# Layer 0 from an unnormalized, transposed x; the norm's per-token factor applied to q, k and v

## The chip, the cores and the metric

The kernel runs on one core of a Trainium2 chip. A core has a matrix engine (TensorE, "PE" in the profile, with its weight loads as "PEld"), VectorE ("DVE"), ScalarE ("ACT"), GpSimd ("POOL") and SyncE ("SP"), which here issues all transfers. The engines run side by side, each through its own list of instructions in order, and wait for one another by semaphores. The metric is the device time of one execution in microseconds; lower is better.

## The reference

A decoder trunk of two layers works on x with 256 tokens and 1024 channels, all in float32. What bears on the change is the beginning of a layer:

```python
h = x * rsqrt(mean(x*x, axis=-1) + 1e-6) * norm_mix_pre     # one factor per token, one weight per channel
proj = h @ w_in                                             # 1024 x 7168
q, k, v, g_ret, sc_b, sc_c, sc_x, cf_a, cf_b, gate_logits = split(proj)
q, k = rotary(q), rotary(k) / 8                             # then retention over chunks of 128 with v
```

Behind it come three branches (retention with a head norm and a gate, a short gated convolution, a convolution of 31 taps with a layer norm), which are merged by sigmoid gates and multiplied with `w_o`, a norm and a residual sum, and then a gated MLP of width 2816 with a convolution of 3 taps, again with a norm ahead of it and one behind it. Since the norm's factor is one number per token, it may be multiplied into h, or into the rows of h @ w_in.

## The kernel before

*Precision.* Every float32 operand of a large product is split into a high part (a rounded copy, type float32r) and a low part (the rest). A product is three matmuls: high by high, low by high, high by low. For activations this is `split` (L173 on ScalarE for the high part, L174 on VectorE for the low part).

*Weights.* All weights are packed into 142 units a layer, each 128 x 1024 (512 KB), in the order of use. The class `Weights` moves them: `dma` (L78) loads a unit into one of 4 raw buffers, `pump` splits it (L105 on ScalarE, L106 on VectorE; in two halves for the units in `HALF`, the first twelve among them), into one of 9 pairs `whi`, `wlo`. Units are prepared up to 8 ahead of use (`LOOK`); `rel` gives a unit back after its last matmul and lets the next one be prepared.

*Beginning.* x comes in two tiles of 128 tokens, tokens on partitions (`xs`). For the first tile, `prenorm` takes the sum of squares on ScalarE (L218), the factor by a power on GpSimd (L211), and multiplies x by factor and weight on VectorE (L236); the weight was broadcast over the partitions by a transfer (L193). `to_hT` turns it into channels on partitions with eight transposes on TensorE (L244) and splits it. Ahead of this TensorE does 12 matmuls on zeros (L199).

*q, k and v.* Four units hold the weights of q and k, four those of v; unit k holds channels 256 k to 256 k + 255. `xs_unit` does a unit's six matmuls for one tile of tokens (L328 to L330, 512 columns each). The first tile's q and k come first; the second tile's transposes come ahead of v. `rotary` (L374 to L386) multiplies q and k by cosine and sine on VectorE, and turns them with four transposes (L384). v is copied by ScalarE (L415).

*Then.* From unit 8 on the weights are the stationary operand: `ws_block` does 24 matmuls of 256 columns (L273, L276) for 128 output channels, with hT as the moving operand. The first of them belong to the 31-tap convolution, whose taps (L425 on VectorE) run in the background of the later blocks; so do the retention's steps (L468 to L501) and the layer norm's.

*Order.* The functions write instructions in the order of the text, but the framework rearranges each compute engine's list by its own planning of when inputs are ready: in the trace, transposes of the second tile stand between matmuls of q that the text has earlier. SyncE's transfers stand in the order of the text.

## Time and profile before

| | us |
|---|---|
| median of 3 runs | 857.51 (856.72 to 858.87) |
| the profiled execution's own span | 855.0 |
| TensorE busy, matmuls | 841.3 (98%) |
| TensorE busy, weight loads | 784.0 (92%) |
| VectorE busy | 654.8 (77%) |
| ScalarE busy | 458.9 (54%) |
| GpSimd busy | 17.9 (2%) |
| matmuls of q, k, v begin | 11.80 |
| last of the 40 slices of TensorE that is not full | 834 to 855 |

An engine's busy time is a share of one profiled execution. The profile also cuts the span into 40 slices with the busy share of each engine in tenths, follows the chain of work that ended last, and groups instructions by line, operation and tile (`whi<-raw` writes tile whi from tile raw). A tile's name is the one in the program. Times in a trace run from the start of the span.

### The profile page before, as it was taken

How to read it: one execution, taken by the hardware profiler on the slowest of the kernel's cores; microseconds unless marked ns; L12 is line 12 of the kernel's file. 1: busy time of each engine (PE TensorE's matmuls, PEld its weight loads, DVE VectorE, ACT ScalarE, POOL GpSimd, SP SyncE). 2: the span in 40 equal slices, each digit the busy share in tenths (PEclk: the TensorE clock that was granted, in tenths of full speed). 3: DMA queues.
4: the chain of work that ended last, by engine and by line, in shares of the span. 5: the costliest groups of instructions: out<-in, count | busy, mean ns of one | idle time of the engine just before them, and what ended most of it. 6: DMA issues, size and time to landing. Idle time of an engine off the chain costs nothing.

```text
span 855.0 us, 14841 instructions
## 1 busy us (share of the span) xinstructions
PE 841.3 (98%) x5868; PEld 784.0 (92%) x5868; DVE 654.8 (77%) x1078; ACT 458.9 (54%) x696; POOL 17.9 (2%) x28
## 2 busy tenths in 40 slices
PE   7999999999999999999999999999999999999997
PEld 4898999999879999999879899999997899999995
DVE  5889999674877976766695999995577698767652
ACT  5654454464666655455655536444647575555541
POOL 0000100000010000000010000000000000000000
PEclk8999999999999999999999999999999999999999
DMA  7885456655665566555466545656556556566511
GB/s 267 301 285 165 157 178 182 191 165 183 217 197 173 176 195 191 178 181 193 169 221 199 173 149 164 184 194 185 166 169 213 176 179 197 172 191 189 187 50 50
DMA packets 43702, 157.13 MB, mean 184 GB/s; under 512 B 4848, under 2 KB 5104, under 8 KB 43632
## 3 DMA queue, kind: packets, MB, share of 16 engines
q1 hardware_dynamic: 43632, 156.18, 57.6%
q8 instruction: 46, 0.75, 0.4%
q14 instruction: 24, 0.20, 0.1%
HBM read 155.12 MB, written 1.05 MB: 183 GB/s over the span
## 4 chain that ended last, share of the span: by engine, by line
PE 95%; DVE 1%; DMA 1%; issue 1%; POOL 1%; ACT 0%; SPq 0%; DVEq 0%; POOLq 0%; ACTq 0%
PE mm L273 36%; PE mm L276 18%; PE mm L313 5%; PE ac L339 5%; PE ac L341 5%; PE ac L343 5%; PE ac L328 4%; PE ac L329 4%; PE ac L330 4%; PE mm L318 3%; PE mm L244 1%; DMA raw<-w_dram 1%; DVE wlo L106 1%; POOL tn L211 1%; PE ac L468 0%
## 5 line engine op out<-in xcount | busy, mean ns | idle before, releaser
L105 ACT ACTIVATE whi<-raw 128x1024 fp32r<-128x1024 f32 (+1 forms) x320 | 296.6, 940 | 299.3 <-PE mm L273 164.0
L106 DVE TENSOR_TENSOR wlo<-raw,whi 128x1024 fp32r<-128x1024 f32 (+1 forms) x320 | 341.4, 1076 | 128.4 <-ACT whi L105 124.3
L273 PE MATMUL mm<-act,whi 128*128 128x256 f32 x2560 | 334.5, 283 | 0.0
L273 PEld LDWEIGHTS mm<-act,whi 128*128 128x128 f32 x2560 | 319.3, 192 | 2.2 <-ACT whi L105 0.7
L276 PE MATMUL mm<-act,wlo 128*128 128x256 f32 x1280 | 179.7, 283 | 0.0
L276 PEld LDWEIGHTS mm<-act,wlo 128*128 128x128 f32 x1280 | 165.1, 192 | 0.0
L425 DVE SCALAR_TENSOR_TENSOR big<-big,par 128x229 f32<-128x229 f32 (+27 forms) x240 | 97.3, 469 | 0.0
L699 DVE SCALAR_TENSOR_TENSOR sm<-mm,par,sm 128x254 f32<-128x254 f32 (+1 forms) x176 | 72.7, 475 | 4.1 <-ACT sm L695 3.8
L339 PE MATMUL ac<-whi,act 128*128 128x512 f32 x228 | 70.7, 391 | 0.0
L341 PE MATMUL ac<-wlo,act 128*128 128x512 f32 x228 | 70.4, 390 | 0.0
L343 PE MATMUL ac<-whi,act 128*128 128x512 f32 x228 | 70.3, 389 | 0.0
L313 PE MATMUL mm<-act,whi 128*128 128x256 f32 x384 | 54.1, 283 | 0.0
L328 PE MATMUL ac<-whi,act 128*128 128x512 f32 x128 | 51.8, 404 | 1.2 <-ACT act L173 1.2
L341 PEld LDWEIGHTS ac<-wlo,act 128*128 128x128 f32 x228 | 42.8, 188 | 9.1
L343 PEld LDWEIGHTS ac<-whi,act 128*128 128x128 f32 x228 | 42.8, 188 | 9.1
L330 PE MATMUL ac<-wlo,act 128*128 128x512 f32 x128 | 50.9, 399 | 0.0
L329 PE MATMUL ac<-whi,act 128*128 128x512 f32 x128 | 50.8, 398 | 0.0
L313 PEld LDWEIGHTS mm<-act,whi 128*128 128x128 f32 x384 | 49.5, 192 | 0.0
L339 PEld LDWEIGHTS ac<-whi,act 128*128 128x128 f32 x228 | 41.4, 188 | 7.3
L695 ACT ACTIVATE sm<-mm,par 128x256 f32<-128x256 f32 x88 | 37.1, 468 | 3.2 <-PE mm L276 2.1
L211 POOL TENSOR_TENSOR tn<-tn,mhalf 128x1 f32<-128x1 f32 (+1 forms) x24 | 17.7, 741 | 832.4 <-DVE tn L221 515.7
L318 PE MATMUL mm<-act,wlo 128*128 128x256 f32 x192 | 30.9, 283 | 0.0
(105 smaller groups left out, 580.0 us busy)
## 6 DMA issues: line engine op xcount, KB each, us to landing
raw<-w_dram SPq DMA_DIRECT2D x284, 512.0 KB, 3.6
gain<-gain_dram SPq DMA_DIRECT2D x7, 512.0 KB, 5.1
xs<-x_dram SPq DMA_DIRECT2D x2, 256.0 KB, 2.7
gain<-gain_dram SPq DMA_DIRECT2D x2, 256.0 KB, 5.7
xs<-x_dram SPq DMA_DIRECT2D x1, 512.0 KB, 9.5
cs<-cst_dram SPq DMA_DIRECT2D x1, 512.0 KB, 6.9
out_dram<-xs SPq DMA_DIRECT2D x1, 512.0 KB, 2.6
out_dram<-xs SPq DMA_DIRECT2D x2, 256.0 KB, 2.1
```

Source lines behind the costliest of these rows:

```text
L105: self.nc.scalar.activation(out=hi[:, s], in_=r[:, s], func=AF.Copy)
L106: self.nc.vector.tensor_tensor(out=lo[:, s], in0=r[:, s], in1=hi[:, s].bitcast(F32), op=ALU.subtract)
L273: nc.tensor.matmul(o, wh[:, kt * P:(kt + 1) * P], rhs_h(hT, kt, hl), start=(kt == 0 and hl == 0), stop=False)
L276: nc.tensor.matmul(o, wl[:, kt * P:(kt + 1) * P], rhs_h(hT, kt, 0), start=False, stop=(kt == NKT - 1))
L313: nc.tensor.matmul(o, wh[:, s], m[:, kt % 2, hl, :], start=(kt == 0 and hl == 0), stop=False)
L328: nc.tensor.matmul(acc, lhs_h(hT, kt, 0, t), wh[:, s], start=(first and j == 0), stop=False)
L329: nc.tensor.matmul(acc, lhs_h(hT, kt, 1, t), wh[:, s], start=False, stop=False)
L330: nc.tensor.matmul(acc, lhs_h(hT, kt, 0, t), wl[:, s], start=False, stop=(last and j == 1))
L339: nc.tensor.matmul(acc[j], lh[:, tsl], hb(wh, j), start=first, stop=False)
L341: nc.tensor.matmul(acc[j], lh[:, tsl], hb(wl, j), start=False, stop=False)
L343: nc.tensor.matmul(acc[j], ll[:, tsl], hb(wh, j), start=False, stop=last)
L425: nc.vector.scalar_tensor_tensor(out=cc_t[:, b, sh:], in0=glu[:, b, :S - sh], scalar=tap, in1=cc_t[:, b, sh:], op0=ALU.mult, op1=ALU.add)
```

## The change

Layer 0 no longer starts from the normalized h. The host also hands in x transposed (channels on partitions), with the weight of the first norm in front of it as a small table `gT` of 128 x 8.

- The transposed x comes in four quarters (`load_xT`), between the first weight units on SyncE's queue. `split_xT` multiplies each block of 128 channels by the norm's weight and splits it in the same instructions: one on ScalarE, one on VectorE. The result is `hT0`, without the per-token factor.
- q, k and v of layer 0 are made from `hT0`, for both tiles of tokens from each unit as it comes (`both`).
- x with tokens on partitions comes later, behind weight 4. From it come the two sums of squares and factors `rs`. `rotary` multiplies q and k by the factor in the instructions that multiply by cosine and sine; the copy of v multiplies by it too.
- For the later stages, the factors are laid out along the free axis on all partitions: a diagonal matrix of the factors on VectorE, multiplied with a matrix of ones on TensorE (`rows`). VectorE multiplies transposed x, norm weight and `rows`, and `split` makes `hT` from it.
- The first four weight units are loaded in two halves. There are 10 instead of 12 matmuls on zeros.
- The tiles of hT hold both tiles of tokens side by side for each channel block, high and low apart, in both layers; layer 1 keeps its way of making them.

```diff
-WARM = 12
+WARM = 10
...
-            self.nc.sync.dma_start(out=r, in_=self.w[self.nd])
+            n = 512 if self.nd < 4 else 1024
+            for c in range(0, 1024, n):
+                self.nc.sync.dma_start(out=r[:, c:c + n], in_=self.w[self.nd][:, c:c + n])
...
+    def load_xT(q):
+        a = xT[q // 2][:, 2 * (q % 2):2 * (q % 2) + 2, :]
+        nc.sync.dma_start(out=a, in_=xt[:, NKT + 512 * q:NKT + 512 * (q + 1)].rearrange("p (a b) -> p a b", b=S))
+
+    def split_xT(q):
+        for j in range(2):
+            kt = 2 * q + j
+            src = xT[kt // 4][:, kt % 4, :]
+            hi, lo = hT0[q][:, j, 0, :], hT0[q][:, j, 1, :]
+            nc.scalar.activation(out=hi, in_=src, func=AF.Identity, scale=gT[:, kt:kt + 1])
+            nc.vector.scalar_tensor_tensor(out=lo, in0=src, scalar=gT[:, kt:kt + 1],
+                                           in1=hi.bitcast(F32), op0=ALU.mult, op1=ALU.subtract)
+
+    load_xT(0)
+    nc.sync.dma_start(out=gT, in_=xt[:, 0:NKT])
+    W.dma(0)
     nc.vector.memset(mhalf, -0.5)
+    ones = const.tile([P, P], F32, name="ones")
+    nc.vector.memset(ones, 1.0)
...
-        return [actp.tile([P, NT, 2, 2, P], F32R, name="act", tag="act") for _ in range(4)]
+        return [act_t() for _ in range(4)]
...
+            def times(out, in0, in1):
+                if rs is None:
+                    nc.vector.tensor_tensor(out=out, in0=in0, in1=in1, op=ALU.mult)
+                else:
+                    nc.vector.scalar_tensor_tensor(out=out, in0=in0, scalar=rs, in1=in1,
+                                                   op0=ALU.mult, op1=ALU.mult)
...
+        if l == 0:
+            def both(k, acc):
+                u = get_xs(k)
+                for t in range(NT):
+                    xs_unit(u, hT0, acc[t], t, k == 0, k == 3)
+                W.rel(u[0])
+
+            for k in range(4):
+                both(k, qa)
+            rs = [rsq(sum_sq([hb(xs[:, t, :], 0), hb(xs[:, t, :], 1)])) for t in range(NT)]
+            both(0, va)
+            both(1, va)
+            rows = mm_t()
             for t in range(NT):
+                dg = sm_t()[:, 0:P]
+                nc.vector.tensor_scalar(out=dg, in0=ident, scalar1=rs[t], scalar2=None, op0=ALU.mult)
+                nc.tensor.matmul(rows[:, t * P:(t + 1) * P], ones, dg, start=True, stop=True)
+            for q in range(4):
+                xn = sm_t()
+                for j in range(2):
+                    kt = 2 * q + j
+                    nc.vector.scalar_tensor_tensor(out=v2(xn)[:, j, :], in0=xT[kt // 4][:, kt % 4, :],
+                                                   scalar=gT[:, kt:kt + 1], in1=rows[:, 0:S],
+                                                   op0=ALU.mult, op1=ALU.mult)
+                split(v2(xn), hT[q][:, :, 0, :], hT[q][:, :, 1, :])
+            rotary(0, qa[0], rs[0])
+            both(2, va)
+            rotary(1, qa[1], rs[1])
+            both(3, va)
+            for t in range(NT):
+                nc.scalar.activation(out=v_s[:, t, :], in_=va[t], func=AF.Identity, scale=rs[t])
+        else:
...
     hT = new_hT()
-    xg = prenorm(0, g_pre0)
-    to_hT(0, xg, hT)
-    W.pump(1)
-    nc.sync.dma_start(out=xs[:, 1, :], in_=x[P:S, :])
-    W.pump(3)
-    xg = prenorm(1, g_pre0)
-    nc.sync.dma_start(out=cs[:, C_COS:C_DEC], in_=cst[:, C_COS:C_DEC])
+    for q in range(4):
+        if q:
+            load_xT(q)
+        split_xT(q)
+        W.pump(q)
+    nc.sync.dma_start(out=cs[:, :C_DEC], in_=cst[:, :C_DEC])
+    for t in range(NT):
+        nc.sync.dma_start(out=xs[:, t, :], in_=x[t * P:(t + 1) * P, :])
     W.pump(LOOK)
...
```

More of the change, by code (lines that the diff above doesn't have):

```diff
@@ L124, in block_kernel @@
 @with_exitstack
-def block_kernel(ctx: ExitStack, tc: tile.TileContext, x, w, gains, par, cst, out):
+def block_kernel(ctx: ExitStack, tc: tile.TileContext, x, xt, w, gains, par, cst, out):
     nc = tc.nc
@@ L179, in block_kernel @@
     mhalf = const.tile([P, 8], F32, name="mhalf")
-    for j in range(2):
-        nc.sync.dma_start(out=xs[:, 0, j * 512:(j + 1) * 512], in_=x[0:P, j * 512:(j + 1) * 512])
     def load_gain(l, k):
@@ L187, in load_gain @@
         return g
-    nc.sync.dma_start(out=cs[:, :C_COS], in_=cst[:, :C_COS])
-    g_pre0 = gp.tile([P, D], F32, name="gain", tag="gain")
-    for j in range(2):
-        sl = slice(j * 512, (j + 1) * 512)
-        nc.sync.dma_start(out=g_pre0[:, sl], in_=gains[0, 0:1, sl].broadcast_to([P, 512]))
+    gT = const.tile([P, NKT], F32, name="gT")
+    xT = [big_t([4, S]) for _ in range(2)]
+    hT0 = [act_t() for _ in range(4)]
+    def load_xT(q):
[12 more added lines that the diff above has]
+    W.dma(0)
     nc.vector.memset(mhalf, -0.5)
+    ones = const.tile([P, P], F32, name="ones")
+    nc.vector.memset(ones, 1.0)
     warm = const.tile([P, 512], mybir.dt.bfloat16, name="warm")
@@ L249, in to_hT @@
                 tl = hT[2 * b + q]
-                split(pv[:, 2 * q:2 * q + 2, :], tl[:, t, :, 0, :], tl[:, t, :, 1, :])
+                c = slice(t * P, (t + 1) * P)
+                split(pv[:, 2 * q:2 * q + 2, :], tl[:, :, 0, c], tl[:, :, 1, c])
     def postnorm(t, acc, gain, order=(1, 0)):
@@ L366, in get_xs, with rotary @@
             return u
-        def rotary(t, ps):
+        def rotary(t, ps, rs=None):
             a = sm_t()
@@ L404, in layer @@
-        rotary(0, qa[0])
-        for k in range(2):
-            xs_unit(uv[k], hT, va[1], 1, k == 0, False)
-            W.rel(uv[k][0])
-        rotary(1, qa[1])
-        for k in range(2, 4):
-            u = get_xs(k)
-            for t in range(NT):
-                xs_unit(u, hT, va[t], t, False, k == 3)
-            W.rel(u[0])
-        for t in range(NT):
-            nc.scalar.activation(out=v_s[:, t, :], in_=va[t], func=AF.Copy)
+        if l == 0:
[10 more added lines that the diff above has]
+            rows = mm_t()
+            for t in range(NT):
+                dg = sm_t()[:, 0:P]
[16 more added lines that the diff above has]
+        else:
+            uq = [get_xs(k) for k in range(2)]
+            for k in range(2):
+                xs_unit(uq[k], hT, qa[0], 0, k == 0, False)
+            uq += [get_xs(k) for k in range(2, 4)]
+            for k in range(2, 4):
+                xs_unit(uq[k], hT, qa[0], 0, False, k == 3)
+            uv = [get_xs(k) for k in range(2)]
+            for k in range(2):
+                if k == TR1:
+                    to_hT(1, xg1, hT)
+                xs_unit(uv[k], hT, va[0], 0, k == 0, False)
+            for k in range(4):
+                xs_unit(uq[k], hT, qa[1], 1, k == 0, k == 3)
+                W.rel(uq[k][0])
+            rotary(0, qa[0])
+            for k in range(2):
+                xs_unit(uv[k], hT, va[1], 1, k == 0, False)
+                W.rel(uv[k][0])
+            rotary(1, qa[1])
+            for k in range(2, 4):
+                u = get_xs(k)
+                for t in range(NT):
+                    xs_unit(u, hT, va[t], t, False, k == 3)
+                W.rel(u[0])
+            for t in range(NT):
+                nc.scalar.activation(out=v_s[:, t, :], in_=va[t], func=AF.Copy)
@@ L812, in block_kernel @@
     nc.sync.dma_start(out=ps_, in_=par)
+    xg = None
     for l in range(L):
```

37 lines of the change are left out of this document (12 added, 25 removed).

## The prediction

> **What bounds the kernel now.** I read the page first: engine shares, the 40 slices, the chain that ended last.
>
> ```profile
> span 855.0 us, 14841 instructions
> PE 841.3 (98%) x5868; PEld 784.0 (92%) x5868; DVE 654.8 (77%) x1078; ACT 458.9 (54%) x696; POOL 17.9 (2%) x28
> PE   7999999999999999999999999999999999999997
> PE 95%; DVE 1%; DMA 1%; issue 1%; POOL 1%; ACT 0%; SPq 0%; DVEq 0%; POOLq 0%; ACTq 0%
> ```
>
> TensorE is the bound everywhere but in the first slice (21.4 us) and the last. The change works in the first, so next I read the instructions in order of time there (start, length, engine, line, operation; in brackets the idle time before it and what ended it).
>
> ```profile
> 1.22 5.30 PE L199 MATMUL mm<-warm 128*128 128x512 bf16 x12 [1.22 <-DVE warm L196]
> 3.07 1.50 SPq L78 DMA_DIRECT2D raw<-w_dram  x3
> 3.27 0.63 ACT L218 ACTIVATE junk<-xs 128x512 f32<-128x512 f32 x1 [1.25 <-DMA xs<-x_dram]
> 4.09 0.63 ACT L218 ACTIVATE junk<-xs 128x512 f32<-128x512 f32 x1
> 7.13 0.75 DVE L236 SCALAR_TENSOR_TENSOR big<-xs,tn,gain 128x512 f32<-128x512 f32 x1 [2.07 <-DMA gain<-gain_dram]
> 9.13 0.75 DVE L236 SCALAR_TENSOR_TENSOR big<-xs,tn,gain 128x512 f32<-128x512 f32 x1 [1.25 <-DMA gain<-gain_dram]
> 10.33 1.15 ACT L105 ACTIVATE whi<-raw 128x512 fp32r<-128x512 f32 x2 [5.51 <-DMA raw<-w_dram]
> 11.80 0.79 PE L328 MATMUL ac<-whi,act 128*128 128x512 f32 x1 [1.20 <-ACT act L173]
> ```
>
> x itself is there by 3.3 us, but the gain, broadcast over the partitions, ends two waits at 7.1 and 9.1 us, and the first weight, queued behind it, arrives at 10.3 us. The first real matmul starts at 11.80 us. From there TensorE runs without a gap (the chain of waits, in order of time):
>
> ```profile
> 13.48 0.43 PE ac L328
> 14.76 0.43 PE ac L328
> 19.27 0.44 PE mm L244 x4
> 30.64 0.23 PE ac L328
> 33.36 0.23 PE ac L328
> 34.49 0.44 PE mm L384 x4
> 38.38 1.92 PE mm L273 x16
> ```
>
> and the granted clock, from busy time by stretch (columns: stretch, length, PE, PEld, DVE, ACT and POOL busy, clock, DMA share, GB/s):
>
> ```profile
> 2.00:3.00 1.00, 1.00 (x4) 0.40 (x3) 0.00 (x0) 0.02 (x1) 0.00 (x0) 1.00 0.92 320
> 11.00:12.00 1.00, 0.20 (x1) 0.20 (x1) 0.90 (x2) 1.00 (x3) 0.00 (x0) 0.50 1.00 410
> 17.00:18.00 1.00, 1.00 (x5) 0.77 (x5) 0.91 (x2) 0.56 (x2) 0.06 (x1) 0.81 0.68 269
> ```
>
> A 512-column matmul takes 0.43 us at clock 0.50 (13.48 to 14.76 is three) and 0.227 at full clock (30.64 to 33.36 is twelve). The clock goes up inside 17:18; a mean of 0.81 puts it at 17.4, that is 5.6 us after 11.80. The q, k, v stage is 8 weight units of 12 such matmuls, 96 in all, plus four groups of four transposes (L244, L384) at 0.44: 96 x 0.227 = 21.8, the slow clock 5.6/2 = 2.8, transposes 1.8, sum 26.4, which from 11.80 gives 38.2, and the first block of the next stage (L273) stands there (its sixteen, 1.92 long, run from about 38.2). So the number to forecast is when that block starts afterwards; what follows is the same work on a full TensorE, and I carry the shift to the end.
>
> **Part by part.** *Taken away before the first matmul:* the broadcast gain loads, the sum of squares, the multiplication L236, eight transposes. In their place stands a transposed x of 256 KB, a small gain table, and the first weight in halves of 256 KB. The transposed x has the size and the queue place of the first half of x, used at 3.27; the second half of x was usable by 4.09. The weight's first half comes third, one such size later: at the 320 GB/s of 2:3 that is 0.8 us, so 4.9. Its high part (half of the 1.15 in L105) is there at 5.5. Ten warm matmuls at 5.30/12 = 0.44 from 1.3 (one more memset ahead) end at 5.7, so TensorE is the later one: real work starts at 5.7 instead of 11.80, 6.1 earlier. The gain table's rows of 32 bytes have no like in the trace; between no time and the 2 us of the wait at 7.13, I take none, because it carries 4 KB; the warm matmuls cover 1 us of it.
>
> *The clock.* Sustained work now begins at 1.3, since warm and real matmuls touch. With the 5.6 us seen after 11.80 the clock is up at 6.9; only 1.2 us of real work is slow and costs 0.6 instead of 2.8. (Bounds: up at 5.7, 0; up 5.6 us after 5.7, 2.8.) The printed clock of 1.00 in 2:3 is no grant: the warm matmuls go at the slow spacing.
> The Trainium skill ("TensorE: Matmul & The Clock Gate", The HAM clock gate) says that a free-running window of 3.4 us must be busy before the clock doubles; by it the estimate is between 4.7 and 8.1, a loss of 0 to 1.2, and the sum moves by 0.6 at most. The trace's 5.6 lies inside the 3.4 to 6.8 which that rule allows.
>
> *Stage work on TensorE.* Eight transposes go (they are not in front either now), eight of rotary stay (0.9), two small fp32 matmuls for `rows` come. Their nearest row is the scores times v, in the chain:
>
> ```profile
> 88.32 0.22 PE ac L491 x2
> ```
>
> 0.2 for two. Sum: 5.7 + 21.8 + 0.6 + 0.9 + 0.2 = 29.2 if nothing is late. That is 9.0 earlier than 38.2.
>
> *What may be late: the normalized hT.* The next stage needs all of hT, now made on VectorE after `rows`: eight multiplications of 128x256 and four subtractions of 128x512. It shares VectorE with the low parts of the weights. Durations (VectorE groups from 3 to 38.3 us by form, the shapes of L174 in the whole trace, L425 in order of time):
>
> ```profile
> L106 DVE TENSOR_TENSOR wlo<-raw,whi 128x512 fp32r<-128x512 f32 x24 | 15.6, 686 | 1.8 <-ACT whi L105 1.6
> L236 DVE SCALAR_TENSOR_TENSOR big<-xs,tn,gain 128x512 f32<-128x512 f32 x4 | 3.0, 750 | 4.0 <-DMA gain<-gain_dram 3.3 <-POOL tn L211 0.7
> L378 DVE TENSOR_TENSOR sm<-ac,cs 128x256 f32<-128x256 f32 x4 | 1.6, 416 | 0.0
> L174 DVE TENSOR_TENSOR act<-sm,act x30: 683/685/693, 111.5 to 831.0; 128x512 fp32r<-128x512 f32 x30
> 52.97 1.66 DVE L425 SCALAR_TENSOR_TENSOR big<-big,par 128x255 f32<-128x255 f32 x4
> ```
>
> 8 x 0.415 + 4 x 0.685 = 6.1 us for hT; a unit's low part is 2 x 0.65 = 1.3. `rows` comes behind unit 5, at 5.7 + 0.6 + 6 x 2.72 = 22.6. The rate at which weights come sets where VectorE is then (stretches of 5 us):
>
> ```profile
> 10.00:15.00 5.00, 3.80 (x12) 2.81 (x13) 3.91 (x8) 4.67 (x11) 0.00 (x0) 0.56 0.82 310
> 30.00:35.00 5.00, 5.00 (x25) 4.14 (x24) 4.79 (x10) 1.26 (x4) 0.00 (x0) 1.00 1.01 373
> ```
>
> Ahead of and with weight 8 go the transposed x (1.05 MB), x (1.05), constants (0.16) and nine weights of 0.52: 7.0 MB, from 1.6 us at 310 or 373 GB/s done at 24.1 or 20.3; I take 22, and its low part is done 1.5 later, at 23.5. Weight 5, 5.4 MB in, is there at 16.1 to 19.1 and needed at 5.7 + 0.6 + 5 x 2.72 = 19.9; with 1.2 for its high part TensorE waits 0.4 at worst, which I leave out since hT is later anyway. From 23.5 VectorE has 6.1 for hT: ready at 29.6, and since the block reaches the last quarter of hT after 12 of its matmuls (1.4 us), it could start at 28.2, ahead of TensorE's 29.2: stall 0. But weights 9 to 11 also land then, 3.9 us of low parts. How VectorE mixes such work is seen where rotary waits before:
>
> ```profile
> 27.07 0.69 DVE L374 TENSOR_TENSOR sm<-ac,cs 128x512 f32<-128x512 f32 x1
> 27.80 1.29 DVE L106 TENSOR_TENSOR wlo<-raw,whi 128x512 fp32r<-128x512 f32 x2
> 29.58 1.29 DVE L106 TENSOR_TENSOR wlo<-raw,whi 128x512 fp32r<-128x512 f32 x2 [0.48 <-ACT whi L105]
> 30.79 0.42 DVE L378 TENSOR_TENSOR sm<-ac,cs 128x256 f32<-128x256 f32 x1
> 31.36 1.29 DVE L106 TENSOR_TENSOR wlo<-raw,whi 128x512 fp32r<-128x512 f32 x2
> 32.57 0.42 DVE L378 TENSOR_TENSOR sm<-ac,cs 128x256 f32<-128x256 f32 x1
> 33.02 0.69 DVE L381 TENSOR_TENSOR sm<-sm 128x512 f32<-128x512 f32 x1
> ```
>
> Rotary's 2.2 us take from 27.07 to 33.7, with the three weights between. So I take all three ahead of hT's end: 23.5 + 3.9 + 6.1 - 1.4 = 32.1, a stall of 2.9. With rotary of the first tile (0.75 + 2 x 0.42 + 0.69 = 2.3; the new form with a scalar is priced as L236) mixed in too it is 34.4, a stall of 5.2. Taken: 2.9, bounds 0 and 5.2.
>
> *Covered.* ScalarE's eight extra high parts stand in the time in which it waited 5.51 for the weight; uncovered, they cost TensorE 0.4 each, as VectorE's do. VectorE's eight low parts of the transposed x (0.42 each) lie between landings before 16 us. SP issues a transfer in 0.5 (L78: three in 1.50), so its 17 up to x are out by 9 us, ahead of the data. x itself now comes behind weight 4, at 14.8 to 17.3 (4.9 MB); from the first square to the factor took 3.9 before (3.27 to 7.13), the second tile adds four pieces' half, 1.7, so both factors stand at 20.4 to 22.9, ScalarE's weights between them excepted, against 22.6 for `rows`. Extra DMA: 1.05 MB of transposed x less 0.52 of gain, hidden as long as weight 5 is in time. The store of hT with both tokens side by side is the same count of instructions and elements: 0. After the stall VectorE owes rotary and the low parts of about two weights, some 5 us; weights are held up to eight units ahead of use, and VectorE is 88% and then 57% busy from 150 us on:
>
> ```profile
> 150.00:160.00 10.00, 10.00 (x86) 10.00 (x85) 8.80 (x14) 4.59 (x5) 0.00 (x0) 1.00 0.60 185
> 160.00:170.00 10.00, 10.00 (x86) 10.00 (x85) 5.69 (x6) 3.68 (x4) 0.00 (x0) 1.00 0.63 200
> ```
>
> so the debt is paid there. If that cover failed, at most those 5 us would come back on TensorE.
>
> *Sum.* The next stage starts at 29.2 + 2.9 = 32.1 instead of 38.2: 6.1 less. The profiled execution spans 855.0, so 848.9; the runs' median 857.51 is 2.5 above that span, and I carry the same 2.5: 851.4.
>
> **Rivals.**
>
> *Nothing is late.* VectorE puts weights 9 to 11 behind hT: 9.0 less, 848.5. For it: no unit needs them then. Against: the mix at 27 to 34 us.
>
> *hT later, and the clock drops.* Rotary goes in too, stall 5.2, and TensorE idles so long that it restarts at half clock, as after the idle stretch before 11.80; a restart there cost 2.8. Together 9.0 - 8.0 = 1.0 less: 856.5. The Trainium skill (same page and section) gives an idle window of 3.4 us as enough for the drop; in this trace the clock was 0.50 at 11.80 after 5.3 us with only eight transposes in it.
>
> *Slower: `rows` waits behind the weights.* Its input needs x's sums of squares on ScalarE and two diagonals on VectorE, which the text places behind low parts up to weight 13. Weights 12 and 13 come behind three more transfers; before, weight 12 was waited for (ScalarE, in order of time):
>
> ```profile
> 36.26 1.06 ACT L105 ACTIVATE whi<-raw 128x1024 fp32r<-128x1024 f32 x1 [0.70 <-DMA raw<-w_dram]
> ```
>
> TensorE stands in order, so units 6 and 7 stand behind `rows`, and hT 6.1 behind it. If the order on VectorE is the text's, `rows` comes at about 36, hT's last quarter is reachable at 36 + 6.1 - 1.4 = 40.7, and a restart at half clock costs 1.4 to 2.8: about 43, which is 4.8 slower, 862.3. It decides from `rows` at 38.2 - 4.7 = 33.5 on. Against: the engines do not keep the text's order; in the same trace ScalarE takes weight 0 (10.33) ahead of the first high part of hT, written earlier.
>
> *The clock rises late.* If the touching warm-up doesn't count, 2.2 more: 853.6; inside the forecast's own range.
>
> **Numbers.** Forecast with stall 1 to 4.5 (849.5 to 853.6): 0.50. Nothing late: 0.18. Late and slow clock: 0.20. Slower: 0.12. About 0.3% (2.6 us) can be told from no change. Forecast and nothing-late are faster; of the third, spread from 853.5 to 858, a third is: faster 0.74. Same: the rest of it and a little of the fourth, 0.16. Slower 0.10. Range: 847.8 (nothing late, clock at once) to 857.5, which leaves out the slower case and the top of the third.
>
> **What would show it.** First matmul of q at 5.5 to 6; granted clock full by 8; `rows` near 23 between two units; the first L273 near 32, with a gap of about 3 us ahead of it ended by VectorE's low part of hT, weights 9 to 11 among hT's work; the rest as long as before. Wrong would be: a first L273 after 36, a gap ahead of `rows`, idle TensorE within units 0 to 5 ended by a weight's DMA, or a second stage that has grown longer.

## The result, and the profile after

The changed kernel takes 864.36 us (median of four runs, 863.03 to 864.99) against 857.70 for the kernel before in the same comparison. The ratio is 1.0076, with a 95% interval of 1.0063 to 1.0088: slower by 0.8%. The forecast was 851.4 us in a range that ended at 857.5, so the time lies outside it, on the other side.

The page of the profile after, with the lines that answer to those of before (span, busy time of TensorE and the others, TensorE in 40 slices, the chain that ended last by engine):

```profile
span 863.2 us, 14826 instructions
PE 840.8 (97%) x5854; PEld 783.9 (91%) x5854; DVE 659.2 (76%) x1089; ACT 463.4 (54%) x700; POOL 17.9 (2%) x28
PE   8499999999999999999999999999999999999996
PE 91%; DVE 1%; issue 1%; POOL 1%; ACT 0%; DVEq 0%; POOLq 0%; ACTq 0%
```

Slice 1 is fuller than before (8, not 7), but slice 2, from 21.6 to 43.2 us, is 4 tenths full where it was at least 9. The later slices are full as before, up to the last (6, not 7). So the beginning gained and something right behind it lost more. Some instructions from the start of the kernel after, in order of time (start, length, engine, line, operation; in brackets the idle time before it and what ended it):

```profile
1.36 4.45 PE L215 MATMUL mm<-warm 128*128 128x512 bf16 x10 [1.36 <-DVE warm L212]
3.85 1.28 ACT L201 ACT_TABLE_LOAD   x1 [3.85 <-DMA gT<-xt_dram]
5.96 1.13 ACT L107 ACTIVATE whi<-raw 128x512 fp32r<-128x512 f32 x2
6.63 0.80 PE L344 MATMUL ac<-whi,act 128*128 128x512 f32 x1 [0.82 <-ACT whi L107]
10.56 0.39 PE L344 MATMUL ac<-whi,act 128*128 128x512 f32 x1
24.87 0.60 PE L428 MATMUL mm<-sm,ones 128*128 128x128 f32 x4
```

The first matmul of q starts at 6.63 instead of 11.80, so 5.2 us of the start are really saved. `rows` (L428) comes at 24.87 and TensorE doesn't wait for it. TensorE around the end of the q, k and v stage:

```profile
30.54 0.39 PE L346 MATMUL ac<-wlo,act 128*128 128x512 f32 x1
41.99 1.11 PE L406 MATMUL mm<-cs,sm 128*128 128x128 f32 x4 [11.06 <-DVE sm L403]
42.75 0.78 PE L344 MATMUL ac<-whi,act 128*128 128x512 f32 x1
45.17 1.11 PE L406 MATMUL mm<-cs,sm 128*128 128x128 f32 x4 [0.36 <-DVE sm L403]
45.93 3.07 PE L289 MATMUL mm<-act,whi 128*128 128x256 f32 x16
```

This is the loss. From 30.9 TensorE stands for 11.06 us, and what ends the wait is not hT but L403, the sum in `rotary` of the first tile. Its four transposes (L406) are next in TensorE's list. Behind them stand four matmuls of the gate (L344, L345), the second tile's transposes and only then the first block of the next stage (L289), at 45.93. (q, k and v were complete: the trace has all their 96 matmuls before 30.9. The gate has 48; the other 44 follow from 69.96 on.) Before, that block (L273) started at 38.22. The rest is nearly unchanged: 863.2 - 45.93 = 817.3 us from there to the end, and 855.0 - 38.2 = 816.8 before. So of the 8.2 us by which the two profiled executions differ, 7.7 are in the place of this one block. (The medians differ by 6.7: the profiled execution of before was the fastest of its four.)

VectorE in the same time, some of its instructions in order:

```profile
25.51 0.48 DVE L433 SCALAR_TENSOR_TENSOR sm<-big,gT,mm 128x256 f32<-128x256 f32 x1 [0.79 <-PE mm L428]
25.91 1.29 DVE L108 TENSOR_TENSOR wlo<-raw,whi 128x512 fp32r<-128x512 f32 x2
27.50 1.29 DVE L108 TENSOR_TENSOR wlo<-raw,whi 128x512 fp32r<-128x512 f32 x2
29.31 1.29 DVE L108 TENSOR_TENSOR wlo<-raw,whi 128x512 fp32r<-128x512 f32 x2
31.40 1.29 DVE L108 TENSOR_TENSOR wlo<-raw,whi 128x512 fp32r<-128x512 f32 x2 [0.41 <-ACT whi L107]
35.78 1.14 DVE L395 SCALAR_TENSOR_TENSOR sm<-ac,tn,cs 128x512 f32<-128x512 f32 x2
36.84 1.22 DVE L108 TENSOR_TENSOR wlo<-raw,whi 128x1024 fp32r<-128x1024 f32 x1
37.98 0.68 DVE L176 TENSOR_TENSOR act<-sm,act 128x512 fp32r<-128x512 f32 x1
38.58 1.22 DVE L108 TENSOR_TENSOR wlo<-raw,whi 128x1024 fp32r<-128x1024 f32 x1
40.11 1.22 DVE L108 TENSOR_TENSOR wlo<-raw,whi 128x1024 fp32r<-128x1024 f32 x1
41.24 0.69 DVE L403 TENSOR_TENSOR sm<-sm 128x512 f32<-128x512 f32 x1
```

L108 is the low part of a weight, L433 and L176 make hT, L395 and L403 are rotary. VectorE is hardly idle here; it works on other things first. Weight 8, the only one that the first block needs, is done at 27.2. Weights 9 to 11 (27.50, 29.31, 31.40) and 12 (36.84) stand between the parts of hT, 13 and 14 (38.58, 40.11) between those of rotary. hT is complete at 38.66 and the first block has all it needs, but rotary's sum ends only at 41.93, and L406 holds the place in front. ScalarE does the same once: it makes the high part of weight 12 (35.75) ahead of that of hT's last quarter (36.72).

The granted clock after, by stretch (the columns as in the prediction: stretch, length, PE, PEld, DVE, ACT and POOL busy, clock, DMA share, GB/s):

```profile
33.00:34.00 1.00, 0.00 (x0) 0.00 (x0) 1.00 (x4) 0.72 (x2) 0.00 (x0) 1.00 1.00 381
34.00:35.00 1.00, 0.00 (x0) 0.00 (x0) 1.00 (x3) 0.54 (x1) 0.00 (x0) 0.68 1.03 422
47.00:48.00 1.00, 1.00 (x7) 1.00 (x6) 0.00 (x0) 0.00 (x0) 0.00 (x0) 0.50 0.75 291
48.00:49.00 1.00, 1.00 (x10) 1.00 (x10) 0.00 (x0) 0.00 (x0) 0.00 (x0) 0.99 0.99 401
```

It falls to half at 34.36 (a mean of 0.68 is 0.36 us at full and the rest at half), 3.4 us after TensorE stops at 30.93, and is up again at 48.0, six microseconds after TensorE resumes. So part of the delay is slow work and not waiting; the experiments have to part the two.

### The profile page after: what moved, and what is told of

The parts are those of the page before. It is cut to its first block, busy times and chain, and to the rows that moved or that the text cites. A ratio compares the mean times of both kernels' runs of the same rounds, so it can differ in the third digit from the quotient of the medians.

```text
span 863.2 us, 14826 instructions
## 1 busy us (share of the span) xinstructions
PE 840.8 (97%) x5854; PEld 783.9 (91%) x5854; DVE 659.2 (76%) x1089; ACT 463.4 (54%) x700; POOL 17.9 (2%) x28
## 4 chain that ended last, share of the span: by engine, by line
PE 91%; DVE 1%; issue 1%; POOL 1%; ACT 0%; DVEq 0%; POOLq 0%; ACTq 0%
PE mm L289 36%; PE mm L292 18%; PE mm L329 5%; PE ac L355 5%; PE ac L357 5%; PE ac L359 5%; PE ac L346 3%; PE ac L344 3%; PE ac L345 3%; PE mm L334 3%; PE mm L260 1%; DVE wlo L108 1%; POOL tn L227 1%; PE ac L522 0%; PE ac L542 0%
## 5 line engine op out<-in xcount | busy, mean ns | idle before, releaser
L108 DVE TENSOR_TENSOR wlo<-raw,whi 128x1024 fp32r<-128x1024 f32 (+1 forms) x320 | 341.9, 1078 | 129.7 <-ACT whi L107 125.8
L289 PE MATMUL mm<-act,whi 128*128 128x256 f32 x2560 | 335.5, 284 | 0.0
L289 PEld LDWEIGHTS mm<-act,whi 128*128 128x128 f32 x2560 | 320.2, 192 | 2.1 <-ACT whi L107 0.7
L292 PE MATMUL mm<-act,wlo 128*128 128x256 f32 x1280 | 179.7, 283 | 0.0
L292 PEld LDWEIGHTS mm<-act,wlo 128*128 128x128 f32 x1280 | 165.1, 192 | 0.0
L344 PE MATMUL ac<-whi,act 128*128 128x512 f32 x128 | 51.9, 406 | 0.8 <-ACT whi L107 0.8
L345 PE MATMUL ac<-whi,act 128*128 128x512 f32 x128 | 51.1, 399 | 0.0
L359 PEld LDWEIGHTS ac<-whi,act 128*128 128x128 f32 x228 | 42.8, 188 | 9.1
L346 PE MATMUL ac<-wlo,act 128*128 128x512 f32 x128 | 50.1, 395 | 0.0
L355 PEld LDWEIGHTS ac<-whi,act 128*128 128x128 f32 x228 | 41.4, 188 | 7.3
L344 PEld LDWEIGHTS ac<-whi,act 128*128 128x128 f32 x128 | 24.8, 194 | 6.8 <-ACT whi L107 1.7
```

The lines of the kernel that those rows point to most:

```text
L108: self.nc.vector.tensor_tensor(out=lo[:, s], in0=r[:, s], in1=hi[:, s].bitcast(F32), op=ALU.subtract)
L289: nc.tensor.matmul(o, wh[:, kt * P:(kt + 1) * P], rhs_h(hT, kt, hl), start=(kt == 0 and hl == 0), stop=False)
L292: nc.tensor.matmul(o, wl[:, kt * P:(kt + 1) * P], rhs_h(hT, kt, 0), start=False, stop=(kt == NKT - 1))
L344: nc.tensor.matmul(acc, lhs_h(hT, kt, 0, t), wh[:, s], start=(first and j == 0), stop=False)
L345: nc.tensor.matmul(acc, lhs_h(hT, kt, 1, t), wh[:, s], start=False, stop=False)
L346: nc.tensor.matmul(acc, lhs_h(hT, kt, 0, t), wl[:, s], start=False, stop=(last and j == 1))
```

## The experiments

The theory after the first look is **order**: nothing is missing in amount, but two lists are in a bad order. On VectorE the low parts of weights that are used later stand ahead of hT and rotary; on TensorE rotary's transposes, whose results nobody needs soon, stand ahead of the next stage's blocks. The rivals are **clock** (the drop to half speed is the main cost), **idle VectorE** (it has nearly no work from 17 to 21 us, while ScalarE makes the sums of squares, and falls behind there), **amount** (VectorE has too much work, in whatever order) and **small edits** (the split loads, the fewer warm matmuls, the new layout of hT cost something by themselves).

In kernels with inserted lines the numbers shift: L292, L295 or L293 is then the block of L289 and L292, L347 to L349 the matmuls of q, k, v and the gate (L344 to L346), L409 or L410 rotary's transposes (L406). "First block" is the start of the first matmul of the next stage, "waits" the sum of TensorE's waits from 12 to 55 us.

| | median us | ratio to before (95%) | first block | waits, ended by |
|---|---|---|---|---|
| before | 857.7 | 1 | 38.2 | none |
| the change | 864.36 | 1.0076 (1.0063 to 1.0088) | 45.9 | 11.4, rotary |
| weights behind | 859.74 | 1.0015 (1.0000 to 1.0029) | 38.4 | 6.3, rotary |
| rotary behind | 855.47 | 0.9972 (0.9956 to 0.9987) | 30.4 | 3.5, hT |
| both behind | 854.04 | 0.9948 (0.9933 to 0.9964) | 30.7 | 2.8, weights and rotary |
| rotary behind, other PSUM tiles | 854.27 | 0.9963 (0.9948 to 0.9978) | 30.3 | 2.7, hT |
| both behind, other PSUM tiles | 850.50 | 0.9923 (0.9905 to 0.9941) | 30.3 | none |

### Both orders, one at a time and together

*Weights behind.* No weight beyond unit 8 is split before hT and rotary are written. (`cap` bounds `pump`, so the high parts on ScalarE and the transfers of these weights move too, not only the low parts.)

```diff
     W.pump(LOOK)
+    W.cap = 8
...
             both(3, va)
+            W.cap = None
+            W.pump(W.cur - 1 + LOOK)
```

> The low parts of weights 9 and later are put behind hT and both rotaries on VectorE; nothing else moves. Theory (VectorE's list holds TensorE up: weights that no unit needs yet stand ahead of hT and of rotary): in the changed kernel low parts of weights 8 to 14 took 8.8 us between 25.5 and 41.2 us; without those of 9 to 14 the first rotary transpose (L406) comes at about 35 instead of 42.0 and the first block of the next stage (L289) at about 38.5 instead of 45.9, so about 857 us. Rival 1 (late weights by DMA hold it up): weights 9 to 12 come no earlier, TensorE's wait stays near 11 us, 864 us. Rival 2 (the start is not the cause at all, something in the later stages is): under 2 us less, 862 to 865 us.

Measured: 859.74. TensorE, in order of time:

```profile
34.95 1.11 PE L409 MATMUL mm<-cs,sm 128*128 128x128 f32 x4 [4.74 <-DVE sm L406]
37.60 1.11 PE L409 MATMUL mm<-cs,sm 128*128 128x128 f32 x4 [1.53 <-DVE sm L406]
38.37 3.76 PE L292 MATMUL mm<-act,whi 128*128 128x256 f32 x16
```

The wait falls from 11.4 to 6.3 us, but it is still rotary that ends it. The first block comes 7.6 us sooner, but the span gains only 5.3 and the median 4.6: from 38.37 to the end it is 819.5, where it was 817.3 after and 816.8 before. The cause is the clock, which was at half from about 33 to 43: sixteen matmuls of the block take 3.56 (38.37 to 41.93) where they take 1.92 at full speed, and the eight behind them 1.58 (to 43.51) instead of 0.96. These are 2.3 of the 2.7 us by which this run is longer than before from the block to the end. This much of the rival "clock" is true.

*Rotary behind.* Both tiles of rotary are written behind the first four blocks of the convolution. The weights stay ahead of hT.

```diff
-            rotary(0, qa[0], rs[0])
             both(2, va)
-            rotary(1, qa[1], rs[1])
             both(3, va)
...
+            if l == 0 and j == 0:
+                for t in range(NT):
+                    rotary(t, qa[t], rs[t])
```

> Both rotaries of layer 0 are moved behind the first four blocks of the next stage; weights stay ahead of hT. Theory (TensorE stands in order behind rotary's transposes, though hT was ready at 38.7 us): the gap then ends with hT, the first L289 comes at about 36 to 37 instead of 45.9, 855 to 857 us. Rival (the order on TensorE does not matter, VectorE's total work does): rotary is still owed, TensorE stops again behind the four blocks for what was gained, 862 to 864 us.

Measured: 855.47, faster than before. The block starts at 30.36 and now waits for hT, in pieces of 1.87, 0.22, 0.57 and 0.84:

```profile
33.34 0.50 PE L289 MATMUL mm<-act,whi 128*128 128x256 f32 x2 [1.87 <-ACT act L175]
37.95 0.62 PE L289 MATMUL mm<-act,whi 128*128 128x256 f32 x3 [0.84 <-DVE act L176]
```

The sum, 3.5, is the size of stall that the prediction had expected at this place (2.9). So rotary's place makes 8.9 us of the median, and without it the forecast mechanism is what remains. The edit moves rotary on VectorE too, but hT is hardly sooner for it (complete at 37.89 instead of 38.66), so nearly all of this is the place in TensorE's list, with the clock, which stayed full here.

*Both behind.*

```diff
+    W.cap = 8
...
-            rotary(0, qa[0], rs[0])
...
-            rotary(1, qa[1], rs[1])
             both(3, va)
+            W.cap = None
+            W.pump(W.cur - 1 + LOOK)
...
+            if l == 0 and j == 0:
+                for t in range(NT):
+                    rotary(t, qa[t], rs[t])
```

> Both moves together: low parts of weights 9 and later behind hT, rotary behind the first four blocks of the next stage. Theory: hT is ready at about 33 and the first L289 stands at about 32, with a gap of at most 1.5 us, so no drop of the clock; 852 us, 5 below the kernel before. Rival (VectorE has too much work before any order helps: 11.7 us of low parts of weights 0 to 8, 3.5 of transposed x, 6.1 of hT, idle for 8 us until data comes): hT no earlier than 36, 857 us or more.

Measured: 854.04. The first block now starts without a wait, and new waits come twelve microseconds later:

```profile
30.74 3.63 PE L292 MATMUL mm<-act,whi 128*128 128x256 f32 x29
42.26 0.60 PE L409 MATMUL mm<-cs,sm 128*128 128x128 f32 x4
44.38 0.50 PE L347 MATMUL ac<-whi,act 128*128 128x512 f32 x1 [1.53 <-ACT whi L110]
51.03 0.63 PE L409 MATMUL mm<-cs,sm 128*128 128x128 f32 x4 [0.73 <-DVE sm L406]
```

With a third of 0.55 these are 2.8 us. Between the two groups of transposes TensorE has no blocks, but the matmuls of the gate (L347), which use units 16 to 19, ahead of units 12 to 15; these units were not prepared yet. Rotary's transposes and the blocks write their results into one ring of PSUM tiles (`mm_t`), handed out in the order of the text, so no block behind rotary can pass the second tile's transposes. That is a reading of the order; the next run tests it.

### Rotary's transposes in other PSUM tiles

```diff
-            pt = mm_t()
+            pt = mm_t() if rs is None else ac_t()
```

This line on top of both orders:

> Weights 9 and later behind hT, rotary behind the first four blocks, and now rotary's transposes write into the PSUM buffers of the accumulators instead of those of the blocks. In the kernel without the last edit the blocks had four PSUM buffers and two of them were held for rotary, so TensorE went to the gate's units 16 and 17 early and waited 2.1 us for their weights. Theory (that wait comes from the buffers' order): the next blocks follow at once, TensorE waits under 1 us between 31 and 60 us, 851 us. Rival (VectorE's debt has to be paid somewhere): 853 to 854 us, with a wait before rotary's transposes instead.

Measured: 850.50, the fastest of all, 7.2 us under the kernel before and 13.9 under the change as it was made. TensorE:

```profile
6.63 0.50 PE L347 MATMUL ac<-whi,act 128*128 128x512 f32 x1 [0.83 <-ACT whi L110]
10.37 0.50 PE L347 MATMUL ac<-whi,act 128*128 128x512 f32 x1 [0.71 <-ACT act L204]
30.30 4.04 PE L292 MATMUL mm<-act,whi 128*128 128x256 f32 x29
42.20 0.60 PE L409 MATMUL ac<-cs,sm 128*128 128x128 f32 x4
50.61 0.66 PE L409 MATMUL ac<-cs,sm 128*128 128x128 f32 x4
```

Both groups of transposes now lie between blocks, without a wait, and the gate's units come in their turn, at 54.8. VectorE does the same work in the same order up to 44 us in both runs, so the tile was the reason. Of the 3.5 us between the two runs, 0.4 lies ahead of the block and comes from the clock at the start, not from the tile. No run changes the tile and leaves rotary where it stood, so what the ring alone does in the change as it was made is not shown. Of the 7.9 us by which the block is earlier than before (38.22 to 30.30), 6.1 reach the end of the span (855.0 to 848.9): rotary's eight transposes have moved behind the block (0.8), the block's first 29 matmuls take 3.87 (30.30 to 34.17, where the next group starts) instead of 29 x 0.12 = 3.5, and 0.6 I cannot place.

The same line and rotary behind, with the weights left ahead of hT:

> The changed kernel with rotary behind the first four blocks and its transposes in the accumulators' PSUM buffers; weights 9 and later stay ahead of hT. Against the kernel with weights behind hT too (e12) it tells what the order of the weights is worth once rotary is out of the way: hT was complete at 37.9 us there and TensorE waited 3.5 us for its parts; theory 854 us, some 3 above e12; rival (no worth): the same as e12 within 1 us.

Measured: 854.27. So the order of the weights on VectorE is worth 3.8 us against the run above. It is partly a wait and partly the clock:

```profile
33.85 0.50 PE L289 MATMUL mm<-act,whi 128*128 128x256 f32 x2 [2.48 <-ACT act L175]
34.58 5.59 PE L289 MATMUL mm<-act,whi 128*128 128x256 f32 x32 [0.22 <-DVE act L176]
```

2.7 us of waiting, and 32 matmuls that end at 40.0, in 5.4 us instead of 3.84.

### How far behind rotary may go

Both orders, and rotary behind eight blocks instead of four:

```diff
-            if l == 0 and j == 0:
+            if l == 0 and j == 1:
```

> As the kernel with both moves, but rotary stands behind all eight blocks of the next stage instead of the first four. There, TensorE stood still for 2.8 us between 42 and 51 us, because rotary's transposes among the blocks made it take the gate's weights (units 16 to 19) ahead of units 12 to 15, before they had come. Theory (what is left is again order: TensorE is sent to weights that are not there): those 2.8 us go, 851 to 852 us. Rival (VectorE's debt must be paid somewhere): the wait shows up again behind the blocks, 854 us.

Measured: 852.71, ratio 0.9934 (0.9910 to 0.9958); 1.3 under four blocks, within the intervals. The waits at 44 to 51 are gone and one of 2.17 has come at 62.46 ahead of L409. The view gives no releaser for it ("issue"); rotary's sum on VectorE had ended just ahead of it, at 62.36. The clock was at half from 63.9 to 67.3 behind it. With the other PSUM tiles as well:

> As e12, with rotary behind all eight blocks. Theory (rotary must neither block hT nor fall behind the background taps on VectorE, which start at about 50 us): rotary late again waits behind taps, a wait of 1 to 3 us before its transposes, 852 to 853 us. Rival: the same as e12.

Measured: 851.55, ratio 0.9931 (0.9916 to 0.9947), with a wait of 0.96 for rotary's sum at 61.70. So going further behind brings nothing; VectorE then does rotary late, among the weights.

### The rivals

*Clock, first try.* 48 idle matmuls on zeros written behind v, meant to fill the gap.

```diff
             both(3, va)
+            wp2 = mm_t()
+            for _ in range(48):
+                nc.tensor.matmul(wp2, warm[:, 0:P], warm, start=True, stop=True)
```

> 48 matmuls on zeros (10 us at full clock) are put on TensorE in the gap ahead of rotary's transposes; all else as in the changed kernel. It prices the clock: if the half clock from about 34.7 to 48 us costs what the rows say (some 6 us of real work at half speed, so about 3 us), the first L289 stays near 45.5, its sixteen take 1.92 instead of 2.72, and the time is about 861 us. Rival (the clock is not part of it): 864 us.

Measured: 875.19, ratio 1.0192 (1.0156 to 1.0229). A miss: they were put behind rotary's transposes, where they cost their own 11 us, and the gap of 10.95 stayed. The clock came back while they ran, though, and from the block (56.50) to the end it is 816.4, 0.9 less than after the change.

*Clock, second try.* 38 idle matmuls that read hT's first quarter, so that they can't start early and fall into the gap.

```diff
                 split(v2(xn), hT[q][:, :, 0, :], hT[q][:, :, 1, :])
+            wp2 = mm_t()
+            for _ in range(38):
+                nc.tensor.matmul(wp2, hT[0][:, 0, 1, 0:P], hT[0].rearrange("p a b c -> p (a b c)")[:, 0:512], start=True, stop=True)
```

> The changed kernel with 38 idle matmuls of 512 columns (8.6 us) that read hT's first quarter and stand right ahead of the last matmul before rotary's transposes, that is in the gap of 11 us, which the first try with 48 matmuls missed. It prices the clock alone: theory, L406 stays at about 42, the four matmuls, the eight transposes and the first block behind the gap run at full clock instead of half, 1.9 us less, 862.5 us. Rival (the drop of the clock makes up most of the loss of 6.7 us): under 859 us.

Measured: 864.25, ratio 1.0076 (1.0057 to 1.0095): as the change without them.

```profile
30.43 8.79 PE L439 MATMUL mm<-act 128*128 128x512 f32 x38
42.44 0.66 PE L406 MATMUL mm<-cs,sm 128*128 128x128 f32 x4 [3.00 <-DVE sm L403]
```

They fill all but 3.0 us of the gap, and rotary's transposes come at 42.44 instead of 41.99. The clock still fell for a while (0.50 from 43.3 to 46.7), but most of the first block, from 46.39 on, runs at full speed, and 816.5 us remain from there, 0.8 less than after the change. So TensorE isn't late because it is slow: it is late because rotary is. What the half clock costs the changed kernel in all is not measured, but its rows bound it at about 1.4: the block's first sixteen matmuls take 2.91 instead of 1.92 (1.0), and the second tile's transposes 0.76 instead of 0.36 (0.4). The first tile's transposes and the four matmuls of the gate were slow too, but behind them TensorE waited 0.36 for rotary's second sum all the same.

*Idle VectorE.* x is loaded behind three more weights, so that VectorE has weights to split where it was idle.

```diff
     nc.sync.dma_start(out=cs[:, :C_DEC], in_=cst[:, :C_DEC])
+    W.pump(4)
```

> The changed kernel, with the loads of x (tokens on partitions) put behind weights 5 to 7 instead of ahead of them; nothing else. Theory: VectorE stood still from 17.2 to 21.0 us because ScalarE took the squares of x (16.9 to 19.9) ahead of the high part of weight 5; since from 21.0 to 41.9 VectorE is never idle for more than a few tenths and ends TensorE's wait, the wait ends about 3 us earlier, L406 at about 39, 861.5 us. Rival (the wait is set by the order of TensorE and of the weights alone, or `rows` comes later for it): no gain, 864 to 865 us.

Measured: 863.79, ratio 1.0072 (1.0054 to 1.0089), no gain that can be told. The idle time on VectorE moved from 17-21 to 21-25 us, half of `rows` came later (26.59), and rotary's transposes still stood at 41.75 after a wait of 10.9. This rival falls.

*Amount.* The change as it is, but with the four low parts of hT on GpSimd, so that VectorE should lose 2.75 us of work (four of 0.69).

```diff
-                split(v2(xn), hT[q][:, :, 0, :], hT[q][:, :, 1, :])
+                nc.scalar.activation(out=hT[q][:, :, 0, :], in_=v2(xn), func=AF.Copy)
+                nc.gpsimd.tensor_tensor(out=hT[q][:, :, 1, :], in0=v2(xn), in1=hT[q][:, :, 0, :].bitcast(F32),
+                                        op=ALU.subtract)
```

> The changed kernel with one edit: the low part of hT (four subtractions of 128x512, 2.75 us on VectorE) on GpSimd, which is idle there and took 1.5 each in the last run that had them. No order in the text is changed. Theory (amount of work on VectorE between 21 and 42 us sets TensorE's wait): L406 comes 2.7 us earlier, and 861.5 us. Rival (order alone): rotary stands behind the weights as before, 864 us.

Measured: 863.87, ratio 1.0074 (1.0058 to 1.0090).

```profile
37.63 1.12 PE L406 MATMUL mm<-cs,sm 128*128 128x128 f32 x4 [6.97 <-DVE sm L403]
42.14 1.12 PE L406 MATMUL mm<-cs,sm 128*128 128x128 f32 x4 [3.40 <-DVE sm L403]
```

The first tile's transposes come 4.4 us sooner, but VectorE puts weights (38.16 and 39.69) between the pieces of the second tile's rotary, and the wait there grows from 0.36 to 3.40. The waits sum to 10.4 instead of 11.4. The block starts 3.0 sooner (42.91), but 1.7 of that is lost again behind it: the clock was at half until 47, and the gate's four matmuls were not done ahead.

The test is weaker than it was meant to be. While GpSimd subtracted, some operations of VectorE took longer:

```profile
29.42 2.00 DVE L108 TENSOR_TENSOR wlo<-raw,whi 128x512 fp32r<-128x512 f32 x2
34.53 2.49 POOL L437 TENSOR_TENSOR act<-sm,act 128x512 fp32r<-128x512 f32 x2 [0.39 <-ACT act L436]
36.06 1.52 DVE L403 TENSOR_TENSOR sm<-sm 128x512 f32<-128x512 f32 x1
```

The first took 2.00 instead of 1.29 (GpSimd worked from 28.90 to 30.26), the last 1.52 instead of 0.69. So VectorE lost about 1.2 us of work and not 2.75. What speaks against this rival is rather the runs above: with the same work in another order the changed kernel gained 13.9.

*Small edits.* The kernel before, with 10 warm matmuls, the first four weights in halves and the new layout of hT.

```diff
-WARM = 12
+WARM = 10
...
+            n = 512 if self.nd < 4 else 1024
...
+                c = slice(t * P, (t + 1) * P)
+                split(pv[:, 2 * q:2 * q + 2, :], tl[:, :, 0, c], tl[:, :, 1, c])
```

> The kernel before with the small edits alone: 10 instead of 12 matmuls on zeros, the first four weights loaded in halves, hT's tiles with both tiles of tokens side by side. Theory: they weigh nothing, 857 to 858.5 us. Rival (the new layout of hT or the halves slow something that runs in both layers): over 860 us.

Measured: 858.65, ratio 1.0007 (0.9998 to 1.0016). They weigh nothing that can be told.

### An earlier start

Three runs tried to win the 0.9 us that the first matmul was later than forecast. They share an early operation on ScalarE, which loads its table ahead of the wait for gT, the weights behind, and rotary behind the gate's four units.

```diff
     nc.vector.memset(mhalf, -0.5)
+    nc.scalar.activation(out=tn_t(1), in_=mhalf[:, 0:1], func=AF.Identity)
...
             bg(BG_CF)
+        if l == 0:
+            for t in range(NT):
+                rotary(t, qa[t], rs[t])
```

> Weights 9 and later behind hT as before, rotary now behind the gate's four units as well, and one more edit: a first small operation on ScalarE that needs no data, so that the load of its function table (1.28 us, which in the changed kernel stood behind the wait for the gain table until 3.85) is over before the data comes. Theory: the real matmuls begin 0.8 earlier (5.8 instead of 6.6) and the 2.2 us in which TensorE stood before rotary's transposes at 62 us go too: 850 us. Rival (every wait that is taken away comes back as another, since VectorE owes the same work): 852.5 us.

Measured: 859.99, ratio 1.0021 (1.0008 to 1.0035).

```profile
10.39 0.73 PE L348 MATMUL ac<-whi,act 128*128 128x512 f32 x2 [1.19 <-ACT act L204]
67.53 0.63 PE L410 MATMUL mm<-cs,sm 128*128 128x128 f32 x4 [2.62 <-issue]
70.75 1.08 PE L410 MATMUL mm<-cs,sm 128*128 128x128 f32 x4 [2.60 <-DVE sm L407]
```

The first matmul starts at 6.15, 0.5 sooner, and TensorE then waits 1.19 for the second quarter of the transposed x: the start is bound by transfers, not by the table. What made the run slow is the place of rotary. Behind the gate it meets VectorE's taps of the long convolution, two waits of 2.6 come back, and the clock is low between 60 and 80 (0.75 in the mean). Against rotary behind eight blocks the profiled execution is 6.2 us longer, and the two traces account for it: ahead of rotary's transposes TensorE stood 3.1 us longer here (two waits of 2.6 instead of one of 2.17), and the clock was at half from 69.8 to 80.1 instead of from 63.9 to 67.3. TensorE was at work in 9.3 us of the one and 3.4 of the other, so half speed cost 4.7 against 1.7.

The same with the decay table, the taps and the second norm's weight loaded later:

```diff
-    nc.sync.dma_start(out=cs[:, C_DEC:], in_=cst[:, C_DEC:])
-    nc.sync.dma_start(out=ps_, in_=par)
...
+            nc.sync.dma_start(out=ps_, in_=par)
...
+            nc.sync.dma_start(out=cs[:, C_DEC:], in_=cst[:, C_DEC:])
+            g_post = load_gain(l, 1)
```

> As e9, with three transfers (decay table 512 KB, taps 280 KB, a gain of 512 KB), none of them needed before the taps at about 55 us, moved behind weight 16 or later. Theory of late weights: where TensorE or ScalarE still waits for a weight's transfer between 30 and 60 us, up to 3 us (1.3 MB at 400 GB/s) go: 848 to 850 us. Rival (order on the engines, not the transfers, is what held TensorE up): the same as e9 within 1 us.

Measured: 860.58, ratio 1.0043 (1.0028 to 1.0059). The wait for the second quarter is 1.97 instead of 1.19: these transfers weren't in the way.

And the early table with hT's low parts on GpSimd, as above:

> As e9, with the low part of hT (four subtractions of 128x512) on GpSimd instead of VectorE. It tells whether VectorE's work still matters once the order is right: if so, 1 to 2 us less than e9; if hT is then no longer what TensorE waits for, the same as e9; if GpSimd takes longer than the 0.7 us of VectorE by more than the slack, hT comes later and the time is above e9.

Measured: 861.65, ratio 1.0044 (1.0028 to 1.0060). GpSimd needs about 1.6 us for each low part here, and two waits of 0.65 and 0.59 come in the first block. VectorE wasn't freed: its low parts of half a weight took 0.92 us in the mean from 20 to 42 us, where they took 0.68 without GpSimd (the run with the early table), which for fourteen of them outweighs the 2.75. The median is 1.7 above that run, but single executions of the two overlap.

## Why the prediction was wrong

**The step that failed is the stall of 2.9 us ahead of the first block.** The prediction let this block start as soon as hT's last low part allowed, and counted rotary on TensorE as 0.9 us of work ("eight of rotary stay"). It read from the trace of before that rotary's transposes stand among the matmuls of v, and priced rotary's time on VectorE, but only as a mix that makes hT late (the 5.2 of the second rival). That the block, behind rotary's transposes in TensorE's list, can't pass them, and that rotary comes mostly behind hT on VectorE, was left out. By the prediction's own terms the block then needs, behind hT at 33.5, rotary's 2.3 and the low parts of weights 12 to 14 (3.6, at the 1.22 each that the rows of the profile after show): 39.4 for the first tile alone. Measured: hT complete 38.66, first tile's sum 41.93, waits 11.4 instead of 2.9. Taking rotary out of the way gave 8.9 us back, and the wait for hT that then showed was 3.5. The 855.47 of that run lie inside the range forecast, 4.1 above its middle estimate; hT was late there too (37.89 instead of 33.5).

The Trainium skill ("PSUM — Partial Sum Buffer", Engine vs sequencer instructions) says that the queues of VectorE and ScalarE are strict first in, first out, and that matmuls start in program order. The trace agrees: the block had its inputs at 38.66 and started at 45.93, behind both groups of transposes. The prediction used this for `rows` and not for rotary.

The other steps:

- *First matmul at 5.7*: 6.63. The 1.28 us in which ScalarE loads its table stand behind the wait for gT, and gT's 4 KB arrive at 3.85. Off by 0.9; moving it gained nothing, because the second quarter of the transposed x is late by as much.
- *Clock up at 6.9*: in the profiled run at about 10.4, a loss of 1.9 instead of 0.6, inside the bounds given. (By the spacing of the matmuls, 0.43 up to there and 0.23 behind; the printed clock reads 1.00 from the start, as it did for the warm matmuls before.) It mattered little. In the run with both orders and other PSUM tiles the spacing was 0.23 from the first matmul on, TensorE waited 0.71 for the second quarter of the transposed x in its place, and the first block came only 0.4 sooner than with both orders alone (30.30 to 30.74), where the clock rose at 10.5.
- *`rows` at 22.6, no wait*: 24.87, no wait. The rival that ended slower, by `rows` behind the weights, is refuted as a mechanism: its time, 862.3, is near the result for another reason. It put the fault in the right list, VectorE's weights ahead of what layer 0 needs, and at the wrong instruction.
- *Stage end at 29.2*: TensorE had all of q, k and v at 30.8, which is 31.5 with rotary's 0.7. Of the 2.3, start and clock make 2.2.
- *Low part of weight 8 at 23.5, hT at 33.5*: 27.2 and 38.66, so 3.7 of the 5.2 us were lost by weight 8. Behind it VectorE mixed in four weights instead of three and two pieces of rotary. That weights are mixed in at all was forecast, from the mix at 27 to 34 us before.
- *The second rival (stall 5.2, and the clock drops)*: the drop is there, at 34.4, and the stall twice as long. Its price was called 2.8; in the run with the weights behind it was up to 2.7, in the change itself 1.4 at most.
- *The rest as long as before*: 817.3 to 816.8. Nearly right, though two things cancel in it: 1.0 of half clock, and the four matmuls of the gate (0.9) that were done ahead. The edits costed at nothing were nothing that can be told (ratio 1.0007).
- *The sign*: the gain forecast at the start was real. With both orders mended the changed kernel takes 850.5, where 851.4 was predicted without them. That is a coincidence in part: the stall of 2.9 is gone there, and start and transfers take about 2 (30.30, where 29.2 less rotary's 0.9 was forecast).
- *The sums*: a stall of 4.5 gives 853.0 by the prediction's own terms and not 853.6. Of the 2.5 carried from span to median, 1.7 are there in both kernels (856.72 to 855.0, 864.95 to 863.2); the other 0.8 came from a profiled execution that was faster than the median.

What would show it wrong had been written down: "a first L273 after 36". It was at 45.9.

## What to carry to other kernels

When a stage in front gets shorter, ask of each engine's list what the next stage's first instruction stands behind, not only what it reads: work that nobody needs soon (here rotary, and weights prepared ahead) must not stand in front of it, neither on the engine that is the bound nor on the one that feeds it. A change that moves work to an engine "with room" is settled by the order in which that engine does it; moving 2.75 us of it to GpSimd gave nothing that can be told here, the same work in another order (the PSUM tiles' included) 13.9. Tiles that are handed out in turn are an order too: a tile from another ring was worth about 3 us.

## What was not expected of the hardware

- A gap of 2.48 us was enough for the clock to fall. In the run with only rotary behind and other PSUM tiles TensorE did two matmuls, waited another 0.22, went on, and still fell to half speed (stretches as above):

```profile
33.00:34.00 1.00, 0.15 (x1) 0.15 (x2) 1.00 (x4) 0.68 (x2) 0.00 (x0) 1.00 1.03 406
34.00:35.00 1.00, 0.78 (x4) 0.57 (x5) 1.00 (x3) 0.58 (x1) 0.00 (x0) 0.86 1.01 414
35.00:36.00 1.00, 1.00 (x7) 1.00 (x6) 0.91 (x2) 0.14 (x1) 0.00 (x0) 0.50 1.04 426
38.00:39.00 1.00, 1.00 (x10) 1.00 (x9) 1.00 (x3) 0.92 (x2) 0.00 (x0) 0.93 0.07 29
```

  It fell at 34.72 (the mean of 0.86 is 0.72 us at full) and was back at about 38.1, 3.4 us later, which cost 1.6 us over 32 matmuls. With waits of 1.87, 0.22, 0.57 and 0.84 in nearly the same place (rotary behind, other tiles not) the clock stayed at 1.00. The Trainium skill ("TensorE: Matmul & The Clock Gate", The HAM clock gate) says that an idle window of about 3.4 us, counted by a clock of its own, brings the drop. A gap of 2.48 is shorter than that. A window that was only mostly idle would explain it: in the 3.4 us up to the fall TensorE stood for 2.7, and with the waits of 1.87 and 0.22 for 2.1 of the 3.4 us from its first stop on. The fall and the return are one such window apart. That is a reading of two runs; how much idle time in a window is enough is not shown.
- The same warm matmuls, with the same gap of 0.8 us behind them, had the clock full at 6.6 us in one run (both orders, other PSUM tiles; matmuls 0.23 apart) and at 10.5 in another whose start is the same (both orders alone; 0.43 apart up to there).
- GpSimd took 1.3 to 1.6 us for a subtraction of 128x512 for which VectorE takes 0.69, and slowed VectorE meanwhile: low parts of half a weight took 0.92 us in the mean instead of 0.68 (early table, with and without GpSimd).
